# Embedding products ahead of V, sums behind the second V group, the channel matrix and q's scale earlier, in a one-core encoder block

## The chip, the cores and the metric

The kernel runs on one core of one Trainium2 chip. The metric is device time in microseconds: the median of the runs of the whole program. One more run of it was profiled, and all rows shown come from that one. The engines go by the profile's names: PE is TensorE (matrix products; PEld its weight loads), DVE is VectorE, ACT is ScalarE, POOL is GpSimd, SP is the engine whose queue issues most transfers. Every engine works through its own instructions in order, and waits on the others by semaphores.

## The reference

One encoder layer on two sequences of 2048 tokens, 1024 wide, in float32. Attention (8 query heads on 2 key-value heads of width 64) and a Fourier branch run side by side, both are gated, concatenated and projected; then an embedding per token is projected and gated into the stream.

```python
u = _rmsnorm(h, g_norm)
z = u @ w_in                                  # q | k | v | ga | f | gf
...
q = _apply_axial_rope(_rmsnorm(q, g_q), cos, sin)
k = _apply_axial_rope(_rmsnorm(k, g_k), cos, sin)
a = _blocked_gqa(q, k, v) * jax.nn.silu(ga)   # softmax over all 2048 keys
fo = _fourier_branch(f, w_fmix) * jax.nn.silu(gf)
h = h + jnp.concatenate([a, fo], axis=-1) @ w_out
gate = jax.nn.sigmoid(_rmsnorm(h, g_ple) @ w_ple_gate)
return h + (p @ w_ple) * gate
```

A final RMSNorm follows. `_fourier_branch` is the real part of a 2-D DFT over (positions, 64 channels) of each of 8 channel groups, and then a 64 x 64 map per group (`w_fmix`).

## The kernel before, in words

Large products are split into float16 high and low parts, three products for one (`mm`, `SPLIT3`); V, the sums and the DFT are float32. On most engines the order of the instructions is the order in which the program emits them, and a small planner in the program decides that order.

**Projection stage** (`project`). Weights are loaded, their largest value is found (VectorE, then an all-reduce on GpSimd), and they are scaled and split by ScalarE (high half, L334) and VectorE (low half, L335). `weights` is a generator of such steps; `some(wq, 9)` takes nine steps of q's weights. A Newton iteration on VectorE (`newton`, L619 and on) makes the inverse norms of a chunk of rows out of the squares that ScalarE makes (L602). Constants of the Fourier stage are loaded near the end of this stage (`fourier_first`), from a call of `later` in iteration n. The background generator `bg` handles the far weights and, last of all, `channel_map`, which writes the channel matrix `bdd` to DRAM; it comes to its end inside this stage, before iteration n.

**Attention stage** (`attention`, driven by `interleave`). A unit is one tile of 128 queries of one key-value head (4 query heads); there are n = 64 units of 8 steps. In step g = 8u + j TensorE does the scores of a block of 256 keys (L1166, half of the rows at a time, in pairs), and a piece of the maxima for a later unit (L1193, into `ps_m`, which has one buffer; VectorE reduces it, L1201). ScalarE takes exponentials (L1169, two per step), GpSimd adds them up (L1172, L1174). In every fourth step, the heavy one (j = 0 and j = 4), TensorE also multiplies the probabilities of four blocks by V (`pv`, L1229, 32 matmuls, `ps_o`); the group at j = 4 is the first of the unit, the group at j = 0 of the next unit is the second. The sums of exponentials of unit u - 1 (`sums`, L1244) stand ahead of the first group of unit u, in a bank of their own kind (`ps_f`), and `divide` behind them: a reciprocal (L1251) and a product (L1252) on VectorE. One flush later the result is stored (L1255).

**The fill.** In steps that are not heavy, `interleave` lets a second generator add work up to an allowance: FILL = 765 us, shared out over the steps' weights (1, SLOW, RATE, and 0 for a heavy step); what a piece costs, by the program's own estimate, is taken off. The fill is first the second half of the Fourier branch (`fourier2`), then the output projection (`outp`): for each tile t of 128 tokens two slots with `w_out` (out1), two with `w_ple_gate` (out3). A slot has 24 half-row matmuls per half, and the upper half of one slot runs paired with the lower half of the one before (`halves`); pieces end at `STOPS`. Behind an out3 slot ScalarE takes a tanh, and the embedding products are put on a list, `todo`: six full-row matmuls with `w_ple` (`products`, L451, `ps_f`), followed one flush later by two VectorE operations (`last`, L1429 and L1431). `embed` takes them off the list in steps with j = 1, 2 or 7.

**Order by hand.** `defer` puts work on a list that the next step's `flush` emits; `defer_slow` puts long VectorE operations (L1391, L1521, L1535) on another, from which `run_slow` takes two in a heavy step with j = 0 and one at j = 4, ahead of V. `after(ticket)` holds the fill back until something deferred has been emitted. A tile's inputs are loaded (L1368) once both of its units are stored (`ready`). After the last unit the rest of the fill runs alone.

Of the kernel before, what the change touches and what calls it, by code (L numbers as in the profile page):

```python
# [140 lines left out]
class Build:  # L141
    def __init__(self, ctx, tc, a, y):
        self.ctx, self.tc, self.nc = ctx, tc, tc.nc
        self.a, self.y = a, y
        nc = self.nc
        ep = ctx.enter_context
        self.const = ep(tc.tile_pool(name="const", bufs=1))
        self.st = ep(tc.tile_pool(name="st", bufs=2))
        self.psF = ep(tc.tile_pool(name="psF", bufs=1, space=PSUM))
        self.psG = ep(tc.tile_pool(name="psG", bufs=2, space=PSUM))  # L150
        self.grouped, self.last_stores = False, nc.sync
        self.psX, self.nx = None, 0
        self.dq, self.d1, self.nflush, self.bg = None, [], 0, iter(())
        self.slow, self.passed, self.step = [], set(), 0
        self.ahead = iter(())
        self.nw2k = 10
        self.sc = {}
        d = lambda n, s, t: nc.dram_tensor(n, s, t, kind="Internal").ap()
        self.qTd = [d(f"qTd{s}", (NT, 128, 8, 128), F16) for s in range(2)]
        self.kTd = [d(f"kTd{s}", (2, 128, NT // 2, 3, 128), F16) for s in range(2)]  # L160
        self.vd = [d(f"vd{s}", (2, 128, NT, 64), F32) for s in range(2)]
        self.gd = [d(f"gd{s}", (128, NT, 512), F32) for s in range(2)]
        self.gfd = [d(f"gfd{s}", (NT, 128, 512), F32) for s in range(2)]
        self.fod = [d(f"fod{s}", (NT, 128, 512), F32) for s in range(2)]
        self.agd = [d(f"agd{s}", (2, 512, SEQ), F32) for s in range(2)]
        self.bdd = d("bdd", (128, 2, 4, 128), F32)
        self.wd = {}
# [61 lines left out]
    def after(self, ticket, more=0):  # L229
        while self.dq is not None and (ticket[0] is None or self.nflush <= ticket[0] + more):  # L230
            yield None
# [334 lines left out]
    def project(self, P, PU, W, early, later, wkv, wq, wf, wgf, wga, bg, mid):  # L566
# [218 lines left out]
        def iteration(i):  # L785
# [42 lines left out]
            if i == n:  # L828
                later()
# [29 lines left out]
        some(wq, 9)  # L859
# [115 lines left out]
    def fourier_first(self, pool):  # L975

        nc = self.nc
        self.F0 = C, G = {}, {}
        self.cx = pool.tile([128, 128], F32, name="c2x", bufs=1)
        for t in range(FP):  # L980
            C[t] = pool.tile([128, 2, 128], F32, name=f"c2_{t}", bufs=1)
            nc.sync.dma_start(C[t][:].rearrange("p g c -> p (g c)"), self.a["c_dft2"][t])
            for g in range(2):
                G[t, g] = pool.tile([128, 512], F32, name=f"g_in{t}{g}", bufs=1)
                r = 16 * t + 8 * g
                nc.sync.dma_start(G[t, g][:], self.gd[0][r:r + 8].rearrange("r t d -> (r t) d"))
            if t == 0:
                nc.sync.dma_start(self.cx[:], self.a["c_dft2x"])

    def fourier2(self, pool, hook):  # L990
# [42 lines left out]
        def mix(t, fT, fx):  # L1033

            fo = [w2k("fo") for _ in range(2)]
            for y in (1, 0):
# [7 lines left out]
                if y:  # L1044
                    nc.scalar.activation(fo[1][:], ps[:], AF.Copy)
                    step()
                    yield 0.86

            def both():
                for y in range(2):  # L1050
# [16 lines left out]
        nc.sync.dma_start(self.bd[:], self.bdd)  # L1067
# [5 lines left out]
        for t in range(16):  # L1073
# [8 lines left out]
            for i in range(2):  # L1082
                ps = self.bank()
                for r in range(4):
# [3 lines left out]
                                     AF.Copy, scale=self.sc["h_gf"][:])  # L1088
                hook()
# [5 lines left out]
            if t % 8 == 0:  # L1095
# [4 lines left out]
                for r in range(4):  # L1100
# [3 lines left out]
                                     scale=self.sc["h_gf"][:])  # L1104
                yield 0.86
# [18 lines left out]
    def attention(self, kvp):  # L1124
# [94 lines left out]
        def pv(u, j0):  # L1219
# [11 lines left out]
            if j0 + PVG == 8:  # L1231
                if u == last[s, kv]:
                    for b in range(2):
                        del vt[s, kv, b]
                AT[u] = at = pool.tile([128, 2, 128], F32, name="at", bufs=2)
                nc.scalar.activation(at[:].rearrange("p c q -> p (c q)"), o, AF.Copy, scale=self.sc["a_scale"][:])  # L1236
                del O[u]
# [53 lines left out]
        for g in range(8 * n + 7):  # L1291
# [10 lines left out]
            if j == 4:  # L1302
                if u + 1 < n:
                    max_rows(u + 1)
                if u > 0:
                    ps = self.bank()
                    sums(u - 1, ps[:, 0:256])
                    divide(u - 1, ps[:, 0:256])
            heavy = (g - 1) % PVG == PVG - 1 and 0 <= g - 1 < 8 * n
            if heavy:  # L1310
                self.run_slow(1 if j else 2)
                pv((g - 1) // 8, (g - 1) % 8 - PVG + 1)
# [19 lines left out]
    def mix(self, s, out):  # L1332
# [5 lines left out]
        yield from self.after(self.defer(lambda: self.mix_max(s, m)))  # L1338
        ps = self.bank()
# [4 lines left out]
        nc.vector.tensor_scalar(out=m[:], in0=self.ident[:, 0:64], scalar1=r[:, 0:1], scalar2=None, op0=ALU.mult)  # L1344
        yield from self.after([self.nflush])
        ps = self.bank()
        for e in range(2):
            nc.tensor.matmul(ps[64 * e:64 * e + 64, 0:64], self.ones[:], m[:], start=True, stop=True)
        nc.vector.tensor_copy(mm[:, 0:3], ps[:, 0:3])
        yield None  # L1350
        yield from self.after(self.defer(lambda: out.append(self.mix_scale(s, mm))))

    def outp(self, pool0, ow, open_pool):
# [60 lines left out]
        def out3(t, n):  # L1414
            hT = HT[t]

            def fin(ps):
                sl = slice(n * 512, (n + 1) * 512)
                th = pool.tile([128, 512], F32, name="th", bufs=1)
# [3 lines left out]
                def products():  # L1423
# [11 lines left out]
                    ticket = TK[t] = self.defer(last)  # L1435
# [5 lines left out]
        def slot(up, whole):  # L1441
# [14 lines left out]
            if up is not None:  # L1456
                ps = self.group_bank()
                for i, us in enumerate(self.mm(ps[:], up[0], up[1])):
                    yield us
                    yield from embed(i >= 6)  # L1460
# [3 lines left out]
        def embed(now=False):  # L1464

            if todo and (now or self.dq is None or self.step % 8 in (1, 2, 7)):
                todo.pop()()
# [7 lines left out]
        def halves(up, low):  # L1475
            i = n = 0
            for k in range(8):
                for ia, ib in SPLIT3:
# [5 lines left out]
                    if i in STOPS:  # L1484
                        yield 0.216 * (i - n)
                        n = i
                        yield from embed(i >= 18)
# [74 lines left out]
        def along(g, pr):  # L1562

            for us in g:
                for _ in range(round(us / 0.648) if us else 0):
                    next(pr, None)
                poll()
                yield us
# [57 lines left out]
        todo, held, started, due, tm, tk, t4 = [], [], [], [], [], {}, {}  # L1626
# [53 lines left out]
    def run(self):  # L1680
# [92 lines left out]
        def fill():  # L1773
            self.nw2k = NW
            self.small = C0 = fill_stack.enter_context(pool("C0", side="right"))
            with pool("B", side="right") as B:
                self.bd = B.tile([128, 2, 4, 128], F32, name="bd")
# [93 lines left out]
```

## Time and profile before

| what | value |
|---|---|
| median of 3 runs | 2668.47 us (2668.46 to 2668.82) |
| the profiled execution | 2671.73 us |
| its span, first to last instruction | 2670.0 us |
| mean granted TensorE clock | 0.995 of full speed |
| TensorE busy | 2611.3 us, 98% |
| VectorE, ScalarE, GpSimd busy | 1612.9 (60%), 1184.7 (44%), 1630.1 us (61%) |

How to read the rows: in a timeline a row is start, length, engine, line, operation, output <- inputs, shapes and the count of merged instructions; `[1.31 <-DVE a_mx]` means that the engine idled 1.31 us before it, until that. In the list of waits a row is who waited for whom, total us, times, longest. In a window's row the busy time of PE, PEld, DVE, ACT and POOL with instruction counts is followed by the granted clock, the share of DMA time and GB/s. In a group of instructions the two numbers behind the bar are busy us and the mean ns of one. The time of the span can be put against the end, since the engine that is busy nearly throughout, TensorE, also ends last in the chain of work. Matmuls overlap, so the distance from one start to the next, not the length, is what one costs.

### The profile page before, as it was taken

How to read it: one execution, taken by the hardware profiler on the slowest of the kernel's cores; microseconds unless marked ns; L12 is line 12 of the kernel's file. 1: busy time of each engine (PE TensorE's matmuls, PEld its weight loads, DVE VectorE, ACT ScalarE, POOL GpSimd, SP SyncE). 2: the span in 40 equal slices, each digit the busy share in tenths (PEclk: the TensorE clock that was granted, in tenths of full speed). 3: DMA queues.
4: the chain of work that ended last, by engine and by line, in shares of the span. 5: the costliest groups of instructions: out<-in, count | busy, mean ns of one | idle time of the engine just before them, and what ended most of it. 6: DMA issues, size and time to landing. Idle time of an engine off the chain costs nothing.

```text
span 2670.0 us, 49974 instructions
## 1 busy us (share of the span) xinstructions
PE 2611.3 (98%) x20096; PEld 1400.3 (52%) x20096; DVE 1612.9 (60%) x2300; ACT 1184.7 (44%) x1983; POOL 1630.1 (61%) x1376
## 2 busy tenths in 40 slices
PE   6999999999999999999999999999999999999998
PEld 3565655655556654545555544545544544555443
DVE  7756465565555775565675666665665666556634
ACT  4443243433224554544444544445445444544442
POOL 1233342333336885877877877877777877777760
PEclk9999999999999999999999999999999999999999
DMA  8567576676538772222222223322232332232223
GB/s 251 150 163 202 165 217 178 172 185 154 141 74 257 231 219 72 62 77 62 75 67 59 66 69 97 99 64 70 64 90 60 79 77 70 69 79 76 62 76 73
DMA packets 453386, 305.37 MB, mean 114 GB/s; under 512 B 294273, under 2 KB 394817, under 8 KB 453153
## 3 DMA queue, kind: packets, MB, share of 16 engines
q1 hardware_dynamic: 440240, 260.41, 37.9%
q0 software_dynamic: 12912, 41.77, 4.2%
q8 instruction: 157, 2.57, 0.4%
q14 instruction: 77, 0.62, 0.1%
HBM read 149.50 MB, written 86.51 MB: 88 GB/s over the span
## 4 chain that ended last, share of the span: by engine, by line
PE 49%; DVE 2%; ACT 1%; issue 0%; DMA 0%; DVEq 0%; SPq 0%; ACTq 0%
PE ps_g L1481 19%; PE ps_o L1229 12%; PE ps_s L1166 10%; PE ps_m L1193 3%; PE ps_f L451 3%; PE ps_x L451 2%; PE ps_f L1244 1%; DVE h L1521 0%; DVE a_mx L1201 0%; PE ps_g L451 0%; ACT p L1169 0%; DVE h_hl L1535 0%; ACT sq L1502 0%; DVE ps_f L1429 0%; ACT h_hl L1502 0%
## 5 line engine op out<-in xcount | busy, mean ns | idle before, releaser
L1174 POOL TENSOR_TENSOR acc<-acc,p 128x1024 f32<-128x1024 f32 x384 | 919.4, 2394 | 201.0 <-ACT p L1169 161.5
L1201 DVE TENSOR_REDUCE a_mx<-ps_m 128x1 f32<-128x1024 f32 x498 | 609.2, 1223 | 564.5 <-PE ps_m L1193 555.2
L1169 ACT ACTIVATE p<-ps_s,s_scale 128x512 f32<-128x512 f32 x1024 | 647.3, 684 | 652.6 <-PE ps_s L1166 634.9
L1481 PE MATMUL ps_g<-w_pg,hT 64*128 64x512 f16 x2784 | 492.2, 376 | 1.9 <-DVE h L1407 1.1
L1229 PE MATMUL ps_o<-p,v 128*64 128x256 f32 x4096 | 468.2, 381 | 0.0
L451 PEld LDWEIGHTS <-uc 128*128 128x128 f16 x3072 | 301.7, 98 | 310.0 <-issue 20.4
L1166 PE MATMUL ps_s<-q,k 64*128 64x512 f16 x3072 | 433.0, 378 | 6.1 <-ACT p L1169 5.9
L1229 PEld LDWEIGHTS ps_o<-p,v 128*64 128x64 f32 x4096 | 288.8, 137 | 166.7 <-issue 28.5
L1481 PEld LDWEIGHTS <-hT 64*128 64x128 f16 x2784 | 205.0, 94 | 155.4 <-issue 12.4
L1481 PE MATMUL ps_g<-w_wo,mh 64*128 64x512 f16 x1440 | 259.0, 376 | 1.2 <-DVE seen L1447 1.2
L1481 PE MATMUL ps_g<-w_wo,mT 64*128 64x512 f16 x1440 | 256.2, 376 | 0.0
L1166 PEld LDWEIGHTS <-k 64*128 64x128 f16 x3072 | 150.7, 94 | 200.7 <-issue 76.8
L1193 PE MATMUL ps_m<-k,q 64*128 64x512 f16 x996 | 199.9, 377 | 5.1 <-DVE a_mx L1201 4.8
L1172 POOL TENSOR_TENSOR acc<-p,p 128x1024 f32<-128x1024 f32 x64 | 150.7, 2355 | 64.2 <-ACT p L1169 63.6
L451 PEld LDWEIGHTS <-w_ga 128*128 128x128 f16 x1536 | 148.8, 98 | 33.6 <-issue 11.1
L942 POOL DMA_DIRECT2D gfd<-gt x32 | 19.7, 614 | 223.3 <-DVE gt L970 190.1
L1481 PEld LDWEIGHTS <-mh 64*128 64x128 f16 x1440 | 99.8, 94 | 91.2 <-issue 18.4
L1481 PEld LDWEIGHTS <-mT 64*128 64x128 f16 x1440 | 102.7, 94 | 81.3 <-issue 3.8
L1251 DVE RECIPROCAL ps_f<-ps_f 128x256 f32<-128x256 f32 x63 | 110.6, 1756 | 21.2 <-PE ps_f L1244 21.2
L451 PE MATMUL ps_x<-w_f,uc 128*128 128x512 f16 x480 | 105.9, 379 | 0.0
L451 PE MATMUL ps_x<-uc,w_ga 128*128 128x256 f16 x936 | 105.5, 273 | 0.0
L1236 ACT ACTIVATE at<-ps_o,a_scale 128x256 f32<-128x256 f32 x64 | 30.3, 473 | 167.5 <-PE ps_o L1229 167.5
(326 smaller groups left out, 3182.8 us busy)
## 6 DMA issues: line engine op xcount, KB each, us to landing
q<-qTd SPq DMA_DIRECT2D x256, 64.0 KB, 2.3
ag<-agd SPq DMA_DIRECT2D x64, 256.0 KB, 3.3
out<-h POOLq DMA_DIRECT2D x31, 512.0 KB, 3.0
x<-in_x_prompt SPq DMA_DIRECT2D x16, 512.0 KB, 5.2
gfd<-gt POOLq DMA_DIRECT2D x32, 256.0 KB, 2.6
gd<-ge POOLq DMA_DIRECT2D x32, 256.0 KB, 2.8
w_st<-in_w_out SPq DMA_DIRECT2D x32, 256.0 KB, 3.8
agd<-gat POOLq DMA_DIRECT2D x64, 128.0 KB, 2.8
```

The lines of the kernel that those rows point to most:

```text
L451: self.nc.tensor.matmul(ps, lhs(ia, k), rhs(ib, k), start=(i == 0), stop=(i == 3 * ks - 1))
L1166: nc.tensor.matmul(S[u][e][:], w[sl], q[sl].rearrange("p h q -> p (h q)"), start=j == i == 0, stop=i + 1 == len(todo), skip_group_check=True)
L1169: nc.scalar.activation(p[:, e, :], S[u][e][:], AF.Exp, scale=self.sc["s_scale"][:])
L1172: nc.gpsimd.tensor_tensor(out=ACC[u][:], in0=P[u, 0][:], in1=p[:], op=ALU.add)
L1174: nc.gpsimd.tensor_tensor(out=ACC[u][:], in0=ACC[u][:], in1=p[:], op=ALU.add)
L1193: nc.tensor.matmul(ps[c], Q[u][0][sl, h, :], kt[s, kv, half][sl, :, 0, :], start=True, stop=True)
L1201: nc.vector.reduce_max(MX[u][:, h, half, c:c + 1], x, axis=AX.X)
L1229: nc.tensor.matmul(o[64 * f:64 * f + 64], vt[s, kv, c // 8][:, c % 8, :], p[:, e, f], start=(c == 0), stop=(c == 15))
L1236: nc.scalar.activation(at[:].rearrange("p c q -> p (c q)"), o, AF.Copy, scale=self.sc["a_scale"][:])
L1244: nc.tensor.matmul(ps[64 * e:64 * e + 64], self.ones[:], av[:, e], start=True, stop=True)
L1251: nc.vector.reciprocal(r, r)
L1481: nc.tensor.matmul(g[0][:], g[1](ia, k)[sl], g[2](ib, k)[sl], start=a, stop=z, skip_group_check=True)
```

## The change

1. *Products.* In a heavy step, `attention` itself takes one group of embedding products off `todo` (now shared as `self.todo`), right ahead of `pv`, if the one before has been dealt with. Its estimate of 1.48 us is put on `self.owed`, which `along` adds to the next piece of fill. `embed` now takes products only when a second group is waiting, when `middle` asks for them, or after the attention. The tanh gets two buffers (`th`).
2. *Sums.* `pv` runs `sums(u - 1)` behind the second V group of unit u, in the free half of `ps_o`, and defers `divide` by one flush. Only the last unit keeps the old place.
3. *Channel matrix.* `bd` is loaded in `fourier_first`. To make room the constants of tile 1 (`c2`) and one of its inputs (`g_in`) are loaded where `bd` was, at the start of `fourier2`.
4. *q's scale.* `some(wq, 10)` takes one step more: the five VectorE operations of the scale now come ahead of the second `newton`.

The further edits (`del ps`, `box`, `evicted`, the counter of banks) keep track of who holds a PSUM bank.

```diff
             if i == n:
+                self.drain(bg)
                 later()
...
-        some(wq, 9)
+        some(wq, 10)
         newton(None, 1, None)
...
         for t in range(FP):
-            C[t] = pool.tile([128, 2, 128], F32, name=f"c2_{t}", bufs=1)
-            nc.sync.dma_start(C[t][:].rearrange("p g c -> p (g c)"), self.a["c_dft2"][t])
+            if t == 0:
+                C[t] = pool.tile([128, 2, 128], F32, name=f"c2_{t}", bufs=1)
+                nc.sync.dma_start(C[t][:].rearrange("p g c -> p (g c)"), self.a["c_dft2"][t])
             for g in range(2):
+                if t and g:
+                    continue
...
             if t == 0:
                 nc.sync.dma_start(self.cx[:], self.a["c_dft2x"])
+                self.bd = pool.tile([128, 2, 4, 128], F32, name="bd", bufs=1)
+                nc.sync.dma_start(self.bd[:], self.bdd)
...
-        nc.sync.dma_start(self.bd[:], self.bdd)
+        for t in range(1, FP):
+            load_c(t)
+            load_g(t, 1)
...
+                r = O.pop(u)[:, 256:512]
+                if u:
+                    sums(u - 1, r)
                 AT[u] = at = pool.tile([128, 2, 128], F32, name="at", bufs=2)
                 nc.scalar.activation(at[:].rearrange("p c q -> p (c q)"), o, AF.Copy, scale=self.sc["a_scale"][:])
-                del O[u]
+                if u:
+                    self.defer(lambda: divide(u - 1, r))
...
-                if u > 0:
+                if u == n:
                     ps = self.bank()
                     sums(u - 1, ps[:, 0:256])
                     divide(u - 1, ps[:, 0:256])
...
                 self.run_slow(1 if j else 2)
+                if self.todo and self.tk[0] is not None and self.nflush > self.tk[0]:
+                    self.todo.pop(0)()
+                    self.owed += 1.48
                 pv((g - 1) // 8, (g - 1) % 8 - PVG + 1)
...
-                th = pool.tile([128, 512], F32, name="th", bufs=1)
+                th = pool.tile([128, 512], F32, name="th", bufs=2)
...
-            if todo and (now or self.dq is None or self.step % 8 in (1, 2, 7)):
-                todo.pop()()
+            if todo and (now or self.dq is None):
+                yield from self.after(self.tk)
+            if todo and (now or self.dq is None):
+                todo.pop(0)()
                 yield 1.48
...
-                        yield from embed(i >= 18)
+                        yield from embed(len(todo) > 1)
...
+                if us:
+                    us += self.owed
+                    self.owed = 0.0
                 yield us
```

More of the change, by code (lines that the diff above doesn't have):

```diff
@@ L154, in __init__ @@
         self.slow, self.passed, self.step = [], set(), 0
+        self.todo, self.owed, self.tk = [], 0.0, [-1]
         self.ahead = iter(())
@@ L230, in after, with evicted @@
         while self.dq is not None and (ticket[0] is None or self.nflush <= ticket[0] + more):
+            yield None
+    def evicted(self):
+        while self.tk[0] is None:
             yield None
@@ L1045, in mix @@
                     nc.scalar.activation(fo[1][:], ps[:], AF.Copy)
+                    del ps
                     step()
                     yield 0.86
+            box = [ps]
+            del ps
             def both():
+                ps = box.pop()
                 for y in range(2):
@@ L1088, in fourier2 @@
                                      AF.Copy, scale=self.sc["h_gf"][:])
+                del ps
                 hook()
@@ L1104, in fourier2 @@
                                      scale=self.sc["h_gf"][:])
+                del ps
                 yield 0.86
@@ L1308, in attention @@
                     divide(u - 1, ps[:, 0:256])
+                    del ps
+                self.nx += 1
             heavy = (g - 1) % PVG == PVG - 1 and 0 <= g - 1 < 8 * n
@@ L1338, in mix @@
         yield from self.after(self.defer(lambda: self.mix_max(s, m)))
+        yield from self.evicted()
         ps = self.bank()
@@ L1344, in mix @@
         nc.vector.tensor_scalar(out=m[:], in0=self.ident[:, 0:64], scalar1=r[:, 0:1], scalar2=None, op0=ALU.mult)
+        del ps
         yield from self.after([self.nflush])
+        yield from self.evicted()
         ps = self.bank()
@@ L1349, in mix @@
         nc.vector.tensor_copy(mm[:, 0:3], ps[:, 0:3])
+        del ps
         yield None
@@ L1434, in products @@
                     nonlocal ticket
-                    ticket = TK[t] = self.defer(last)
+                    ticket = TK[t] = self.tk = self.defer(last)
                 return products
@@ L1459, in slot @@
                     yield us
-                    yield from embed(i >= 6)
+                    yield from embed(i >= 6 or len(todo) > 1)
                 yield from self.after(ticket)
@@ L1625, in outp @@
         ticket = [-1]
-        todo, held, started, due, tm, tk, t4 = [], [], [], [], [], {}, {}
+        todo, held, started, due, tm, tk, t4 = self.todo, [], [], [], [], {}, {}
         self.grouped = True
@@ L1776, in fill @@
             with pool("B", side="right") as B:
-                self.bd = B.tile([128, 2, 4, 128], F32, name="bd")
                 ow = {}
```

## The prediction

> **What bounds the kernel now.** I read the page's busy times first, then one window over the steady part of the attention stage, then what TensorE waited for, then the timelines of single stretches.
>
> ```profile
> PE 2611.3 (98%) x20096; PEld 1400.3 (52%) x20096; DVE 1612.9 (60%) x2300; ACT 1184.7 (44%) x1983; POOL 1630.1 (61%) x1376
> ...
> 1070.00:2600.00 1530.00, 1523.16 (x13212) 763.37 (x13207) 930.23 (x866) 745.60 (x1226) 1170.60 (x987) 1.00 0.28 73
> ...
> PE ps_x L451 <- ACT wr_q L334: 7.1, 1, 7.1
> ...
> PE ps_g L1041 <- DMA bd<-bdd: 4.8, 1, 4.8
> PE ps_m L1193 <- DVE a_mx L1201: 4.8, 9, 1.3
> ```
>
> TensorE sets the time: 1523.16 of 1530 us busy in the long stage. Its work there is fixed, so a change gains only by dearer-than-needed switches between kinds of matmul or by single waits, and every microsecond in which TensorE is made to wait is added to the end. The two waits that this change names are 7.1 and 4.8 us. The last row matters most below: the maxima (L1193) have one PSUM buffer, so each must wait for VectorE's reduction of the one before (L1201); that costs 4.8 us in all today.
>
> **Embedding products in front of V.** The products are 57 groups of six full matmuls in this form (x342):
>
> ```profile
> L451 PE MATMUL ps_f<-wp,pT 128*128 128x512 f16 x342 | 83.7, 381 | 0.0
> ...
> 1504.43 0.38 PE L1193 MATMUL ps_m<-k,q 64*128 64x512 f16 x2
> 1504.74 1.47 PE L451 MATMUL ps_f<-wp,pT 128*128 128x512 f16 x6
> 1506.14 0.82 PE L1166 MATMUL ps_s<-q,k 64*128 64x512 f16 x6
> 1506.80 0.38 PE L1193 MATMUL ps_m<-k,q 64*128 64x512 f16 x2
> 1507.01 1.46 PE L1481 MATMUL ps_g<-w_wo,mT 64*128 64x512 f16 x12
> ```
>
> Between two kinds that use half rows, a maximum takes 1507.01 - 1506.80 = 0.21 us of TensorE; ahead of a product it takes 1504.74 - 1504.43 = 0.31. The six products take 1506.14 - 1504.74 = 1.40 instead of 6 x 0.216 = 1.30 (twelve half matmuls, six pairs, take the same 1.30). So a group of products pays 0.10 on the way in and 0.10 on the way out. Placed in front of V, the way in remains and one of two ways out is shared: V's own entry. Whether full rows to V's half columns is free the stretch does not show: between 0 and 0.10 saved on top of 0.095, so -5.4 us (57 x 0.095) to -10.8. I take -5.4, because V is again another shape of the array. (The Trainium skill, TensorEngine Tiling (Array Packing), Key Properties, says that changing the tiling mode drains TensorE, while changing the tile does not. Full to half columns is a change of mode, so by that rule the saving is 5.4 and not 10.8; the rows above agree that a change of rows costs about 0.1.)
>
> The price lies in the debt. Before, a product was charged 1.48 to the step in which it ran, where it also gave ScalarE time. Now the charge (owed) falls on the first piece of projection after the V step. A step's allowance is 765 / 420.9 = 1.82 us (the 420.9 is the weighted step count in run), or 2.09 with RATE; the pieces of a slot hold 12, 6, 6, 6, 6, 12 matmuls (STOPS), so in 4 of 6 cases the first piece costs 0.65 + 1.48 = 2.13 and the step ends with six matmuls.
>
> ```profile
> 821.64 0.82 PE L1166 MATMUL ps_s<-q,k 64*128 64x512 f16 x6
> 822.49 1.26 ACT L1169 ACTIVATE p<-ps_s,s_scale 128x512 f32<-128x512 f32 x2
> ```
>
> The exponentials begin 0.85 after the scores and take 1.26: the banks are free 2.11 us after the scores began. Scores 0.65, maximum 0.22 and six matmuls 0.65 fill only 1.51 of that, so TensorE idles 0.60. 57 x 4/6 x 0.60 = **+23 us** (0 if the pieces mostly fall at twelve, 34 if always at six).
>
> **Sums behind the second V group.** Sums and V already stand side by side:
>
> ```profile
> 1523.39 0.65 PE L1244 MATMUL ps_f<-acc,ones 128*64 128x256 f32 x4
> 1523.87 3.62 PE L1229 MATMUL ps_o<-p,v 128*64 128x256 f32 x32
> 1524.63 1.76 DVE L1251 RECIPROCAL ps_f<-ps_f 128x256 f32<-128x256 f32 x1
> 1526.48 0.42 DVE L1252 TENSOR_TENSOR at<-at,ps_f 128x256 f32<-128x256 f32 x1
> ```
>
> so the four matmuls cost the same 0.43 to 0.48 in the new place: 0. What moves is VectorE's work. Today the reciprocal and product (1526.90 - 1524.63 = 2.27 us) run while TensorE does 3.6 us of V. Deferred behind the second group, they come one flush later, in the step after that V, ahead of that step's reduction; nothing long runs on TensorE then. And in that V step run_slow emits two long operations instead of one. This is the place where VectorE is already late:
>
> ```profile
> 1536.65 3.67 PE L1229 MATMUL ps_o<-p,v 128*64 128x256 f32 x32
> 1540.26 0.82 PE L1166 MATMUL ps_s<-q,k 64*128 64x512 f16 x6
> 1540.91 0.38 PE L1193 MATMUL ps_m<-k,q 64*128 64x512 f16 x2
> ...
> 1544.54 0.39 PE L1193 MATMUL ps_m<-k,q 64*128 64x512 f16 x2 [1.31 <-DVE a_mx L1201]
> 1535.63 0.70 DVE L1429 SCALAR_TENSOR_TENSOR ps_f<-th,ps_f 128x512 f32<-128x512 f32 x1 [0.24 <-PE ps_f L451]
> 1536.37 0.75 DVE L1431 SCALAR_TENSOR_TENSOR h<-ps_f,p_wp,h 128x512 f32<-128x512 f32 x1
> ...
> 1538.16 2.98 DVE L1535 SCALAR_TENSOR_TENSOR h_hl<-h,h_r,h_hl 128x1024 f16<-128x1024 f32 x1
> 1541.07 2.29 DVE L1521 SCALAR_TENSOR_TENSOR h<-h,rsh_z,gfin 128x1024 f32<-128x1024 f32 x1
> ```
>
> Here VectorE is busy until 1543.36, 3.1 us past the end of V, and TensorE waits 1.31 us. Put the sums (+0.43 us) and 2.27 us of VectorE's work in this stretch and the reduction starts 2.27 later, the maximum is due 0.43 later: 1.8 us more. Without long operations: the reciprocal starts 0.6 us after V's end, the reduction is done at 0.6 + 2.27 + 1.22 = 4.1 us, and TensorE gets to its second maximum at 0.43 + 0.66 + 0.22 + f + 0.65, with f the projection between: a stall where f is under about 2.1 us. I did this sum for each of the 54 second V groups from here
>
> ```profile
> 1059.60 3.67 PE L1229 MATMUL ps_o<-p,v 128*64 128x256 f32 x32
> ...
> 2502.24 3.67 PE L1229 MATMUL ps_o<-p,v 128*64 128x256 f32 x32
> ```
>
> (the first and the last), with f and VectorE's end as they stand: 24 without a long operation behind V stall 0.22 on average, 16 with one 0.56, 14 with two 1.48: 5.4 + 9.0 + 20.7 = 35, of which about 2.6 are there today: **+32 us**. Where a product ran in front of that V, its two operations (0.70 + 0.75, above) also come ahead of the divide; with them the same sums give 5.4 + 18.7 + 41.0 = 65. About half of the products will fall on a second group: half of the difference, **+15** (0 to 30). No other engine covers any of this: TensorE is in order, and scores and projection stand behind the waiting maximum.
>
> The store of the divided rows also comes 5 steps later; what that may cost is a rival.
>
> **Channel matrix early.** Before, its load stands behind the last k store on SP; two other loads, c2 and g_in of tile 1, now take that place.
>
> ```profile
> 826.69 0.32 SPq L1067 DMA_DIRECT2D bd<-bdd x1
> 823.60 1.06 PE L1085 MATMUL ps_f<-c,g_in 128*128 128x128 f32 x8
> ...
> 830.47 0.79 PE L1041 MATMUL ps_g<-bd,fT 128*128 128x128 f32 x2 [4.85 <-DMA bd<-bdd]
> c<-in_c_dft SPq DMA_DIRECT2D x3, 128.0 KB, 3.4
> 800.00:876.00 76.00, 70.86 (x544) 48.80 (x544) 43.88 (x61) 36.67 (x62) 50.38 (x35) 0.96 0.87 255
> ```
>
> TensorE needs tile 1's c at 823.60, earlier than it needed bd. Issued at 826.69 and 3.4 us on the way, c lands at 830.1: the stall of 4.85 does not go, it moves forward, and the 2.0 us of work between 823.60 and the old stall now comes after it. 830.1 + 2.0 - 830.47 = +1.6; part of that runs at the lowered clock (mean 0.96 in this window), so **+1.8** (0 to +3.6). If c were in time the whole wait and some clock would be saved, -7; that needs an issue 6 us earlier, and SP is not free earlier.
>
> **q's scale sooner.** VectorE leaves the scale chain until behind the second Newton, which waits for ScalarE's squares:
>
> ```profile
> 25.73 0.35 POOL L322 PARTITION_ALL_REDUCE p_mm<-w_m  x1 [9.99 <-DVE n_ms L619]
> 28.45 0.17 DVE L621 TENSOR_SCALAR n_ms<-n_su 128x2 f32<-128x2 f32 x1 [2.79 <-ACT jk L602]
> ...
> 30.91 0.15 DVE L272 TENSOR_SCALAR p_p<-p_mm 128x1 f32<-128x1 f32 x1
> ...
> 32.49 2.74 DVE L335 SCALAR_TENSOR_TENSOR wr_q<-w_z,w_gs,wr_q 128x512 f16<-128x512 f32 x4 [0.79 <-ACT wr_q L334]
> ```
>
> The maximum is ready at 26.1, and the 0.8 us chain fits into VectorE's wait of 2.79. Then ScalarE can split behind its squares, and VectorE's first low half starts when Newton is done, at 31.0 instead of 32.49: **-1.5 us**. The loads behind it on SP move along, so I keep all of it (0 to -2.5).
>
> **Sum**, against the profiled execution of 2671.73 us: -5.4 + 23 + 32 + 15 + 1.8 - 1.5 = +65, so 2737; the median of the runs is 3.3 lower, 2734.
>
> **Rivals.**
> *VectorE has the room* (faster). If f behind the second V group is over 2.1 us nearly everywhere and the debt ends in pieces of twelve, the 70 us are not paid: -5.4 - 1.5 + 1.8 = -5, 2663; with free entry to V and c in time, 2650. For it speaks VectorE's idle share of 40%; against it, the 1.31 us wait above and 30 of 54 groups with long operations. Deciding point: f = 2.1 us. Chance 0.11, and 0.04 that it ends within 0.2% (what a measurement can tell from no change).
> *The debt costs nothing, the divide does* (slower, less): 23 and half of 15 fall away, 2704. For it, ScalarE is idle 51% of the stage. Chance 0.2.
> *The later store starves the projection* (slower, more). Each tile's load stands right behind a store:
>
> ```profile
> 2045.64 0.38 SPq L1255 DMA_DIRECT2D agd<-at  x1
> ...
> 2047.54 0.38 SPq L1368 DMA_DIRECT2D ag<-agd  x1
> 2074.47 1.33 DVE L1391 SCALAR_TENSOR_TENSOR mh<-ag,mix_s,mh 128x1024 f16<-128x1024 f32 x1
> 2075.95 0.38 PE L1481 MATMUL ps_g<-w_wo,mh 64*128 64x512 f16 x1
> ```
>
> This tile is used 1.5 us after its split; five steps of some 3.4 us are 17 us late. In most other tiles I find 14 to 21 us of room. Four bare steps cost about 1.2 us each (2.11 - 0.87); with six such tiles +29, and idle windows that halve the clock for 3.4 us (1.7 us each) may double it: 2763 to 2790. (The Trainium skill, TensorE: Matmul & The Clock Gate, What's actually happening, tells of such a free-running window of 3.4 us; the mean of 0.96 above is of that kind.) Chance 0.15.
> *As forecast:* 0.5, from 2704 to 2765.
>
> The numbers: faster 0.11, same 0.04, slower 0.85. The range leaves out the faster rival and the far end of the worst: 2682 to 2782; the forecast's own is 2704 to 2765.
>
> **What would show it.** Right: TensorE's wait for a_mx (L1201) rises from 4.8 to some 50 us, its wait for p (L1169) to some 25, both right behind a second V group; c instead of bd ahead of L1085 near 823; wr_q's first split at 28.5 on ScalarE. Wrong: those waits under 15 us, or reciprocals that start before V ends.

## The result, and the profile after

The changed kernel takes **2785.93 us** (median of 5 runs, 2779.15 to 2788.06) against 2668.47: a ratio of 1.0429, 95% interval 1.0414 to 1.0443, or +114 us. The forecast was 2734, the end of its range 2782. The direction was right, nearly half of the loss was not in the sum. The profiled execution took 2788.06.

Three views of the changed kernel: the busy times on its page, the waits of TensorE (in all, times, longest), and its busy times in the stretches that the prediction read, with two of the tail (the eighth column is the granted clock).

```profile
PE 2657.8 (95%) x20096; PEld 1430.6 (51%) x20096; DVE 1608.9 (58%) x2300; ACT 1184.4 (43%) x1983; POOL 1630.4 (59%) x1376
```

```profile
PE ps_m L1213 <- DVE a_mx L1221: 39.8, 50, 2.7
PE ps_s L1186 <- ACT p L1189: 34.3, 88, 3.0
...
PE ps_g L1516 <- DVE seen L1480: 6.3, 2, 5.1
PE ps_f L1103 <- DMA c<-in_c_dft: 5.6, 1, 5.6
```

```profile
1070.00:2600.00 1530.00, 1465.39 (x12424) 746.54 (x12420) 881.98 (x828) 705.08 (x1159) 1102.60 (x932) 0.99 0.27 68
...
2600.00:2720.00 120.00, 111.60 (x837) 52.44 (x836) 49.78 (x48) 45.01 (x72) 71.12 (x66) 0.91 0.30 78
2697.10:2717.40 20.30, 17.69 (x41) 5.58 (x41) 7.78 (x10) 3.65 (x5) 1.89 (x2) 0.50 0.55 139
```

In the stretch 1070 to 2600, TensorE's 1523.16 busy us have become 1465.39: 57.8 us lost in the long stage. The wait for the maxima's reduction went from 4.8 to 39.8 us (some 50 were expected), and 39.0 us of it stand behind a second V group, as forecast. The wait for the exponentials went from 8.0 to 34.3 us; its row before the change:

```profile
PE ps_s L1166 <- ACT p L1169: 8.0, 22, 2.3
```

Neither explains TensorE's own 46.5 us of extra "busy" time. Part of that is the clock: the span's mean went from 0.995 to 0.985, which is 28 us over 2786 at most, since TensorE was idle in some of it. What the rest is, the rows do not say. One piece is in the last row: for 20.3 us the tail ran at half the clock, from within a wait for `seen` (VectorE's one-column copy out of a slot's bank), which VectorE reached late:

```profile
2699.71 2.72 PE L1516 MATMUL ps_g<-w_pg,hT 64*128 64x512 f16 x6 [5.14 <-DVE seen L1480]
```

What happens behind a second V group is seen in one stretch of the changed kernel's timeline (start, duration, engine, operation, tiles):

```profile
1141.75 1.47 PE L456 MATMUL ps_f<-wp,pT 128*128 128x512 f16 x6
...
1143.15 3.67 PE L1249 MATMUL ps_o<-p,v 128*64 128x256 f32 x32
...
1147.85 0.38 PE L1213 MATMUL ps_m<-k,q 64*128 64x512 f16 x2
...
1152.88 0.39 PE L1213 MATMUL ps_m<-k,q 64*128 64x512 f16 x2 [2.72 <-DVE a_mx L1221]
```

```profile
1142.99 2.97 DVE L1570 SCALAR_TENSOR_TENSOR h_hl<-h,h_r,h_hl 128x1024 f16<-128x1024 f32 x1
1145.88 2.29 DVE L1556 SCALAR_TENSOR_TENSOR h<-h,rsh_z,gfin 128x1024 f32<-128x1024 f32 x1
1148.10 0.68 DVE L1462 SCALAR_TENSOR_TENSOR ps_f<-th,ps_f 128x512 f32<-128x512 f32 x1
1148.82 0.75 DVE L1464 SCALAR_TENSOR_TENSOR h<-ps_f,p_wp,h 128x512 f32<-128x512 f32 x1
1149.48 1.76 DVE L1275 RECIPROCAL ps_o<-ps_o 128x256 f32<-128x256 f32 x1
1151.27 0.42 DVE L1276 TENSOR_TENSOR at<-at,ps_o 128x256 f32<-128x256 f32 x1
1151.61 1.22 DVE L1221 TENSOR_REDUCE a_mx<-ps_m 128x1 f32<-128x1024 f32 x1
```

This is the queue that the prediction drew: two long operations, the product's two, the divide, and only then the reduction for which the second maximum waits 2.72 us. Product to V takes 1143.15 - 1141.75 = 1.40 us, as product to scores did: the way into V still costs 0.10 (1.40 is also the median of all 56 groups of products in front of V), so one switch is saved and not two. (The Trainium skill, TensorEngine Tiling (Array Packing), Key Properties, says that a change of the tiling mode drains TensorE; by that rule the way from full rows to V's half columns is not free, and this row agrees.)

The stretch that the sum did not contain, in the same timeline:

```profile
1180.94 0.38 SPq L1279 DMA_DIRECT2D agd<-at  x1
1182.84 0.38 SPq L1401 DMA_DIRECT2D ag<-agd  x1
...
1195.69 1.89 PE L1516 MATMUL ps_g<-w_pg,hT 64*128 64x512 f16 x16
1197.42 0.81 PE L1186 MATMUL ps_s<-q,k 64*128 64x512 f16 x6
...
1215.31 2.09 DVE L1424 SCALAR_TENSOR_TENSOR mh<-ag,mix_s,mh 128x1024 f16<-128x1024 f32 x1
...
1217.67 0.39 PE L1516 MATMUL ps_g<-w_wo,mh 64*128 64x512 f16 x1
```

The tile's load again stands 1.9 us behind a store, but it is needed as soon as it is split (1215.31 to 1217.67). From 1197.4 to 1217.6 there is no output projection at all. Stretches of 18 to 22 us like this one begin at 1197, 1507, 1974, 2035, 2094 and 2153 us, with shorter ones between.

### The profile page after: what moved, and what is told of

It reads as the page before. It is cut to its first block, busy times and chain, and to the rows that moved or that the text cites. A ratio compares the mean times of both kernels' runs of the same rounds, so it can differ in the third digit from the quotient of the medians.

```text
span 2785.9 us, 49981 instructions
## 1 busy us (share of the span) xinstructions
PE 2657.8 (95%) x20096; PEld 1430.6 (51%) x20096; DVE 1608.9 (58%) x2300; ACT 1184.4 (43%) x1983; POOL 1630.4 (59%) x1376
## 4 chain that ended last, share of the span: by engine, by line
PE 82%; DVE 10%; ACT 3%; DMA 2%; issue 1%; SPq 1%; POOL 0%; DVEq 0%; ACTq 0%; POOLq 0%
PE ps_g L1516 20%; PE ps_x L456 16%; PE ps_o L1249 15%; PE ps_s L1186 10%; PE ps_g L456 7%; PE ps_f L456 7%; PE ps_m L1213 3%; DVE ps_o L1275 3%; DVE a_mx L1221 2%; ACT p L1189 2%; DVE h L1556 1%; PE ps_o L1268 1%; PE ps_x L931 1%; DVE at L1276 1%; ACT at L1259 1%
## 5 line engine op out<-in xcount | busy, mean ns | idle before, releaser
L1516 PE MATMUL ps_g<-w_pg,hT 64*128 64x512 f16 x2784 | 498.8, 379 | 9.7 <-DVE seen L1480 5.1
L1186 PE MATMUL ps_s<-q,k 64*128 64x512 f16 x3072 | 461.7, 382 | 31.6 <-ACT p L1189 31.4
L1186 PEld LDWEIGHTS <-k 64*128 64x128 f16 x3072 | 164.5, 94 | 239.0 <-issue 120.2
L1213 PE MATMUL ps_m<-k,q 64*128 64x512 f16 x996 | 212.7, 382 | 40.4 <-DVE a_mx L1221 39.8
L1275 DVE RECIPROCAL ps_o<-ps_o 128x256 f32<-128x256 f32 x63 | 111.2, 1765 | 119.9 <-ACT at L1259 119.9
L1516 PEld LDWEIGHTS <-mh 64*128 64x128 f16 x1440 | 105.4, 95 | 86.4 <-issue 22.1
L1516 PEld LDWEIGHTS <-mT 64*128 64x128 f16 x1440 | 111.2, 94 | 65.1 <-issue 0.7
L1213 PEld LDWEIGHTS <-q 64*128 64x128 f16 x1024 | 69.1, 95 | 120.2 <-issue 73.6
```

The costliest lines, as they stand in the source:

```text
L1186: nc.tensor.matmul(S[u][e][:], w[sl], q[sl].rearrange("p h q -> p (h q)"), start=j == i == 0, stop=i + 1 == len(todo), skip_group_check=True)
L1213: nc.tensor.matmul(ps[c], Q[u][0][sl, h, :], kt[s, kv, half][sl, :, 0, :], start=True, stop=True)
L1275: nc.vector.reciprocal(r, r)
L1516: nc.tensor.matmul(g[0][:], g[1](ia, k)[sl], g[2](ib, k)[sl], start=a, stop=z, skip_group_check=True)
```

## The experiments

In what follows a time is the kernel's ratio to the kernel before in the same comparison, times 2668.5 us, with the 95% interval. The theory at the outset: divide, debt and later store each cost by themselves. The rival: one of them makes the loss and the others hide.

**q's scale alone.**

```
-        some(wq, 9)
+        some(wq, 10)
```

> The kernel before with the single change of q's scale (its chain one instruction sooner in the start). The whole change came out 117 us slower; this part is one that I had priced at a gain. Theory A (as forecast): TensorE's first wait for wr_q is over sooner and the rest moves along, -1.5 us (-2.5 to 0) against the kernel before. Theory B (the gain is eaten): in the changed kernel TensorE waits 5.48 us at 30.39 and once more 2.06 us at 33.03 for VectorE's half of wr_q, and half the clock from 27.8 lasted 10.24 us in place of 6.83 us from 29.5; the first scores came 1.2 us sooner in all. Then 0 to -0.8 us here. Both say no slower.

Measured: ratio 1.0000 (0.9991 to 1.0008), 0 us (-2.4 to +2.1). TensorE's waits in that stretch, in this kernel:

```profile
PE ps_x L451 <- ACT wr_q L334: 3.4, 1, 3.4
PE ps_x L451 <- DVE wr_q L335: 2.3, 1, 2.3
```

The first wait is 3.7 us shorter (7.08 before), the second, 0.21 before, is 2.3: VectorE's half is late next. About 1.6 us of gain in the rows, and the times cannot tell that from nothing.

**The channel matrix alone.** The matrix is loaded with tile 0's inputs, two of tile 1's take its old place:

```
+        self.bd = pool.tile([128, 2, 4, 128], F32, name="bd", bufs=1)
+        nc.sync.dma_start(self.bd[:], self.bdd)
...
-        nc.sync.dma_start(self.bd[:], self.bdd)
+        for t in range(1, FP):
+            load_c(t)
+            load_g(t, 1)
```

> The kernel before with the channel matrix loaded early, and nothing else of the change. Theory A (as forecast): the wait of 4.85 us for bd goes and one of about 5.6 us for c of tile 1 comes in its place, 2 us earlier: +1.8 us (0 to +3.6). Rival: the wait is the same length and stands at another place, 0 within 0.5 us, or the clock gets a window less at half, -1.7 us.

Measured: 1.0012 (1.0004 to 1.0021), +3.2 us (1.1 to 5.6). The wait for `bd` is gone, and one for `c` stands in its place, as in the forecast, which had +1.8 (0 to 3.6):

```profile
830.81 1.40 PE L1093 MATMUL ps_f<-c,g_in 128*128 128x128 f32 x5 [5.49 <-DMA c<-in_c_dft]
```

**The sums alone, and the late store alone.** The first is the sums' part of the diff without the products. The second keeps everything of the kernel before and only makes the store wait for five more flushes:

```
-            self.defer(store)
+            def later(k):
+                self.defer(store if k == 0 else lambda: later(k - 1))
+            later(5 if u < n - 1 else 0)
```

> The kernel before with only the sums of exponentials moved behind the second V group, the divide deferred one flush behind it, and so the store of the divided rows five steps later. The products stay where they were and are charged to their own step. Theory A (the divide stands by itself, as the forecast has it): VectorE's reciprocal and product stand ahead of the reduction of the maxima, TensorE's wait for a_mx goes from 4.8 to about 35 us, and the later store adds starved projection of 10 to 25 us: 2705 to 2735. Rival B (debt and divide only cost together): the steps behind V keep all of their projection here, which hides the divide; a_mx stays under 15 us, and the time is within 10 us of the kernel before. Rival C (the store alone): a_mx under 15 us, but projection gaps of some 20 us at several tiles with empty steps, 2690 to 2700.

> The kernel before with only the store of the divided rows made five flushes later (not for the last unit); sums, divide, products and all else as before. Theory A (the later store starves the projection by itself): the room of 14 to 21 us between a tile's split and its first use shrinks to some 0 to 5 us, TensorE has no projection in 15 to 40 steps, each about 1.2 us: +15 to +40, so 2683 to 2708, with more waits for p and more half-clock windows but a_mx as before. Rival B (the room is enough as long as no time is lost elsewhere): within 3 us of the kernel before, the tiles' splits only move closer to their use; the gaps in the changed kernel are then a consequence of its other losses or of where its projection stood.

Measured: the sums alone 1.0310 (1.0294 to 1.0326), **+83 us**, more than theory A's 2735 allows; the late store alone 1.0186 (1.0172 to 1.0200), **+50 us**. Waits and the tail's window of the late store:

```profile
PE ps_s L1166 <- ACT p L1169: 22.1, 59, 2.0
...
PE ps_g L1484 <- DVE mh L1394: 8.5, 8, 1.9
...
PE ps_g L1484 <- DVE seen L1450: 6.3, 2, 5.2
...
PE ps_m L1193 <- DVE a_mx L1201: 3.0, 7, 1.2
```

```profile
2600.00:2721.00 121.00, 106.77 (x574) 46.60 (x570) 42.68 (x96) 28.70 (x44) 27.87 (x34) 0.89 0.30 73
```

The reduction is on time, TensorE even waits for the tile's split itself (`mh`), and the projection has gaps up to 23 us. In 16 of 30 tiles the split's low half begins 3 us or less before the tile's first use; before the change one tile was that tight. The last V matmul starts 38 us later (2624.0 against 2586.0); the other 14 us of this profiled execution (span 2721.7) lie behind it, where the 5.2 us wait for `seen` and a clock of 0.89 stand as in the changed kernel. Rival B is out: this part alone costs as much as the divide and more. The range given for theory A (15 to 40) was still too low.

**A smaller delay.** The same edit with two flushes in place of five.

> The kernel before with only the store of the divided rows later, by two flushes instead of the five of the earlier run (+49 us). Theory A (room: most tiles have 14 to 21 us between split and first use, two steps take about 7 of them): only the few tiles with 1.5 to 7 us of room come late, 0 to +10 us. Rival B (the price grows with each step of delay): 2/5 of 49, +15 to +25.

Measured: 1.0047 (1.0031 to 1.0064), +12.5 us (8 to 17). Two of five steps cost a quarter of the price, between the two expectations. There is room, but it isn't a threshold that the tiles share: p waits are already 16.6 us in place of 8.0, and 9 of 30 tiles have 3 us or less left, where one had before.

**The late divide alone.** The kernel before with the sums in the free half of V's bank, in front of the first V group, and the divide deferred by one flush (the store, which follows the divide, is then one step late, not five):

```
             o = O[u][:, 0:256]
+            if j0 == 0 and u:
+                r = O[u][:, 256:512]
+                sums(u - 1, r)
+                self.defer(lambda: divide(u - 1, r))
```

> The kernel before with only the divide late: the sums stay in front of the first V group, now in the free half of V's bank, and the divide is deferred by one flush, so it follows behind V; the store is one step later, not five. Products as before. Theory A (the divide has a price of its own, 82 us of the sums alone less 49 of the later store): +25 to +35, a_mx about 30 us, no projection gaps over 12 us. Rival B (divide and store cost mostly together): under +15, and then the store's share in the changed kernel is larger than its run alone showed. Rival C: +40 or more, the divide is the larger part.

Measured: 1.0105 (1.0090 to 1.0120), **+28 us** (24 to 32). Without the five steps of the store the divide still costs, and 50 + 28 is nearly the 83 of the sums alone. The 28 contain one step of later store, which no run prices by itself (one gap of 16 us in the projection is there, at 2087 us). But a_mx is only 16.5 us here against 39.9 with the sums alone; the rows of this kernel and of the sums alone:

```profile
PE ps_m L1193 <- DVE a_mx L1201: 16.5, 27, 1.8
```

```profile
PE ps_m L1193 <- DVE a_mx L1201: 39.9, 51, 2.6
```

The timelines show one reason; first this kernel, behind a first V group, then the changed kernel, behind a second one:

```profile
1105.05 0.82 PE L1166 MATMUL ps_s<-q,k 64*128 64x512 f16 x6
1105.16 1.77 DVE L1255 RECIPROCAL ps_o<-ps_o 128x256 f32<-128x256 f32 x1 [2.82 <-PE ps_o L1233]
```

```profile
1202.20 3.67 PE L1249 MATMUL ps_o<-p,v 128*64 128x256 f32 x32
...
1206.24 0.82 PE L1186 MATMUL ps_s<-q,k 64*128 64x512 f16 x6
1206.86 1.77 DVE L1275 RECIPROCAL ps_o<-ps_o 128x256 f32<-128x256 f32 x1 [2.99 <-ACT at L1259]
```

Behind the first group the reciprocal starts 0.11 us after the scores, behind the second 0.62: there it waits for ScalarE to read V's half of the same bank, which in turn waits for the sums.

**The store nearly on time in the changed kernel.** The same edit on the changed kernel, products and debt kept. It brings the store back to one step late, and with it moves the sums and the divide behind the first V group.

> The changed kernel, but the sums of unit u-1 go into the bank of unit u in front of its FIRST V group, where they stood before the change, and the divide is deferred by one flush as in the change. So VectorE's divide still follows behind a V group instead of lying under it, but the store of the divided rows comes one step later than in the kernel before instead of five. Theory A (three separate prices: the later store 49 us, as its run alone showed; the divide about 33, the rest of the run with the sums alone; products and debt about 32): the starved projection and its p waits go, 40 to 50 us come back, and the divide behind a V group with one long operation instead of two gives back some 5 to 10 more of the a_mx wait: 2725 to 2745, a_mx 25 to 35 us. Rival B (the gaps come from the lost time of divide and debt, the store is not needed for them): at most 15 us come back, 2770 or more. Rival C (the store alone makes the loss, divide and debt hide under the room): 2690 or less, a_mx under 15 us.

Measured: 1.0261 (1.0243 to 1.0278), +70 us: **45 us come back**, as theory A has it. a_mx falls by 11.2 us and p by 8.4, so not all of the 45 has to be the store's. The two waits in that kernel:

```profile
PE ps_m L1213 <- DVE a_mx L1221: 28.6, 45, 1.6
PE ps_s L1186 <- ACT p L1189: 25.9, 82, 1.8
```

**The long operations shared out the other way.**

```
-                self.run_slow(1 if j else 2)
+                self.run_slow(2 if j else 1)
```

> The changed kernel with the long operations of VectorE shared out the other way round: one in front of a second V group, where the divide follows, and two in front of a first one, where none does. Theory A (the long operations ahead of the divide make about half of the a_mx wait, 20.7 of 35 us by my sums over the second groups with two): a_mx falls from 39.8 to 20 to 28 us, 10 to 20 us come back, 2766 to 2776. Rival B (the divide with its own 2.3 us is enough for the wait, long operations or not): a_mx stays above 33 us and the time within 5 us. Rival C (an operation now one V group later is late for its tile): slower.

Measured: 1.0412 (1.0396 to 1.0429), 5 us under the changed kernel with overlapping intervals, a_mx 39.6. Rival B: the long operations ahead of the divide do not make half of the wait, although single stretches such as the one at 1152.88 look like it. They make a little: behind the second groups a_mx falls from 39.0 to 34.7 us, behind the first ones, where two long operations stand now, it rises from 0.7 to 4.9.

**The products alone.** The kernel before with only the products' part of the diff.

> The kernel before with only the products moved in front of V, with their debt (any V group); sums, divide and store stay as before. Theory A (my terms: -5.4 for the switches, +23 for the debt, and nothing from the divide, which stays under V): p waits rise from 8 to some 25 us with room in hand, +10 to +25, so 2680 to 2695. Rival B (the debt costs only together with the late divide and the late store): -5 to +3. Rival C: the 32 us between the sums alone and the whole change all lie here, +28 or more.

Measured: 1.0580 (1.0563 to 1.0596), **+155 us**, more than the whole change and far above theory A. Rival C's "+28 or more" holds it in form, but not for its reason. The wait row and one stretch of this kernel:

```profile
PE ps_f L456 <- DVE at L1264: 82.5, 28, 3.8
```

```profile
1096.35 1.76 DVE L1263 RECIPROCAL ps_f<-ps_f 128x256 f32<-128x256 f32 x1
1098.20 0.42 DVE L1264 TENSOR_TENSOR at<-at,ps_f 128x256 f32<-128x256 f32 x1
...
1098.68 2.40 PE L456 MATMUL ps_f<-wp,pT 128*128 128x512 f16 x6 [2.92 <-DVE at L1264]
```

In front of the first V group, beside which the sums take a rotating bank, the product gets that very bank and waits for the divide, 82.5 us in 28 products. The two parts of the change are coupled. The sums' move into V's bank is what lets the products stand in front of the first group without this wait. So the same again with products in front of the other V group only. (`j == 0` is the second group of a unit; where the expectations of this kernel, and of the same one without the debt below, say "a first V group only", the second is meant.)

```
+                if j == 0 and self.todo and self.tk[0] is not None and self.nflush > self.tk[0]:
+                    self.todo.pop(0)()
+                    self.owed += 1.48
```

> The kernel before with the products in front of a first V group only (never in front of the one next to which the sums take a rotating bank), with the debt. Sums, divide and store as before. With products in front of any V group and the sums in their old bank, TensorE had waited 82.5 us in 28 products for VectorE's divide to give the bank back. Theory A (that was the bank alone; what is left is the debt): no waits of products for the divide, p waits of 20 to 27 us, +8 to +25. Rival B: products in front of V cost 100 us or more for another reason, and the time stays above 2780. Rival C (debt for nothing): -5 to +3.

Measured: 1.0111 (1.0096 to 1.0126), **+30 us** (26 to 34), for 43 products, somewhat above theory A. The waits for p have grown as expected; the wait row of this kernel and its busy times:

```profile
PE ps_s L1178 <- ACT p L1181: 21.8, 68, 1.6
```

```profile
PE 2620.8 (97%) x20096; PEld 1418.5 (53%) x20096; DVE 1611.0 (60%) x2300; ACT 1182.8 (44%) x1983; POOL 1627.7 (60%) x1376
```

46 more waits for p list 13.8 us of idle time. The span grew by 27.4 us (2697.4 against 2670.0): TensorE was idle for 17.9 us more, and its busy time as a whole went up by 9.5 us (2620.8 against 2611.3) at the same count of matmuls and a clock of 0.996. Where these 9.5 us come from is not shown.

**Without the debt.** In the changed kernel, in the one with the store nearly on time, and in the one with products in front of a second V group only (there with 43 for 57):

```
-FILL = 765.0
+FILL = 765.0 - 57 * 1.48
...
-                    self.owed += 1.48
```

> The changed kernel without the debt: a product in front of V is charged to no step, and the total to be shared out over the steps is smaller by the same amount (57 x 1.48 us), so the projection is spread evenly. Theory A (the debt makes the steps behind V short, p waits 34 us against 19 with the sums alone): p waits fall to about 20 us and the a_mx wait falls a little as the second maximum is reached later: 15 to 30 us come back, 2756 to 2771. Rival B (the steps are empty because tiles come late, whatever the charge): within 8 us of the changed kernel. Rival C: the projection pulled forward runs into the late store more often, slower than the changed kernel.

> The changed kernel with the sums in front of the first V group in V's bank and the divide deferred (the earlier run of this: 2742, a_mx 28.6, p 25.9 us), now also without the debt, the total smaller by 57 x 1.48 us. Theory A (the debt is a price of its own): p falls to 12 to 18 us and 10 to 20 us come back, 2722 to 2732. Theory B (cover): p falls and a_mx rises by about as much, as in the changed kernel without the debt (p 34.3 to 16.8, a_mx 39.8 to 56.1): within 8 us of 2742.

> The products in front of a first V group only, sums, divide and store as before the change (the earlier run with the debt: +29 us, p waits 21.8 us), now without the debt: a product is charged to no step and the total to be shared out is smaller by 43 x 1.48 us (43 products stood in front of V there). Theory A (the price is the debt, which puts the loss into one step): p waits fall to about 12 us and half or more of the 29 us comes back, 2668 to 2684. Theory B (the price is the cover: 43 products of 1.4 us have gone out of the short steps into a step in which TensorE was busy anyway, and ScalarE's exponentials stay uncovered by as much wherever the charge falls): p and a_mx waits together stay at 22 to 30 us, 2690 to 2705.

Measured: the changed kernel without the debt 1.0390 (1.0372 to 1.0408), 10 us back, between the two theories; with the store nearly on time 1.0134 (1.0119 to 1.0149), **34 us back**, from +70 to +36, more than theory A's 10 to 20. Waits, first of the changed kernel without the debt, then with the store also nearly on time:

```profile
PE ps_m L1213 <- DVE a_mx L1221: 56.1, 61, 2.9
...
PE ps_s L1186 <- ACT p L1189: 16.8, 43, 1.8
```

```profile
PE ps_m L1213 <- DVE a_mx L1221: 30.2, 42, 2.4
...
PE ps_s L1186 <- ACT p L1189: 9.5, 24, 3.0
```

Where tiles arrive in time, the debt is a price of its own: p falls from 25.9 to 9.5 and a_mx stays. Where the store is late, the one wait only turns into the other (74.1 us together with the debt, 72.9 without). The third kernel, 1.0157 (1.0133 to 1.0181), is 12 us *slower* than with the debt, above the ranges of both theories. Its p falls from 21.8 to 9.0 us, but a_mx rises from 7.0 to 12.1, a wait of 10.7 us for `seen` ends at 2626 us, and two waits for `mr` (the transposed maxima) appear, 7.3 us together. It decides nothing: p does what theory A says, a_mx moves as theory B says, and the time follows neither.

**The divide under V again.** The kernel with the store nearly on time, but with the divide called at once instead of deferred.

```
-                self.defer(lambda: divide(u - 1, r))
+                divide(u - 1, r)
```

> The changed kernel with the sums in V's bank in front of the first V group and the divide at once behind them, so that VectorE divides while TensorE does V and the store goes out in the step in which it did before the change. Products in front of V and their debt stay as changed. Theory A (what is left is products and debt, and the coupling of the banks is gone): a_mx under 10 us, p 20 to 30 us, 2680 to 2705. Rival B (VectorE's divide and TensorE's V in one bank wait for each other): V starts 2 us later at each unit, some 63 x 2.2 us: 2800 or more. Rival C: faster than the kernel before, the products' switches are saved and the debt costs nothing.

Measured: 1.1308 (1.1291 to 1.1325), **+349 us**, rival B. The wait row and one stretch:

```profile
PE ps_o L1253 <- DVE at L1276: 213.3, 63, 8.3
```

```profile
1107.17 1.76 DVE L1275 RECIPROCAL ps_o<-ps_o 128x256 f32<-128x256 f32 x1
1108.96 0.42 DVE L1276 TENSOR_TENSOR at<-at,ps_o 128x256 f32<-128x256 f32 x1
...
1109.44 5.36 PE L1253 MATMUL ps_o<-p,v 128*64 128x256 f32 x32 [2.87 <-DVE at L1276]
```

V, in one half of the bank, waits for the divide in the other: 213.3 us over 63 units. The clock falls to 0.957, which is up to 3019.8 x (0.995 - 0.957) = 115 us more. Of the places tried in V's bank, a divide ahead of V costs far more than one behind it, so with the sums there the late divide is the cheaper of the two.

None of these kernels is measurably faster than the kernel before.

## Why the prediction was right and wrong

- **The sum.** Each part alone: late store 50, late divide 28, products with debt 30, channel matrix 3, q 0. Together 111, against +114 for the whole. The theory of separate prices holds to that extent, and part of the closeness is luck: the 30 are for 43 products and not 57, the 28 contain one step of later store, and the debt costs 34 us where tiles come in time but only 10 in the whole change. That the sum without the store (+65) is near the +70 measured with the store nearly on time is luck too: divide and products' operations were put too high (47, the late divide alone measured 28), debt and switches too low (17.6 against 30).
- **The step that failed**: "The store of the divided rows also comes 5 steps later; what that may cost is a rival." It was in the sum with nothing and cost 50 us. The numbers for it were on the page: 17 us late against 14 to 21 us of room. That leaves -3 to +4 us, which is no room, and still I let "most other tiles" count as safe and took six tiles as late. With the late store 16 of 30 had 3 us or less left. Its rival's time (2763 to 2790) holds the result; its chance of 0.15 did not follow from its own arithmetic. What it also lacked is the tail, 14 of the 50 us.
- **Divide, +32**: measured 28. The rival by which VectorE has the room is out. The working inside it was right in part only: the reciprocal does not start 0.6 us after V's end but about 1.0 (1206.86, with V's last matmul done by 1205.87), since it waits for ScalarE's read of the same bank; and the weight given to the long operations (20.7 of 35) fell with their swap, which took 4.3 us of a_mx from behind the second groups.
- **Products' operations ahead of the divide, +15**: not seen where the forecast put them. a_mx is 39.9 us with the sums alone and 39.8 in the whole change. With the divide behind the first group a_mx does grow with the products, from 16.5 us to 28.6, and stays so without the debt (30.2); no run gives this a time of its own.
- **Debt, +23, and switches, -5.4**: 17.6 together, and 30 for 43 products instead of 57. The mechanism was right, and the idle time nearly (13.8 us of p for 43, where 43 x 4/6 x 0.60 is 17.2). Mis-sized was what comes with it: 4.1 us more of other idle time, and TensorE's busy time rose by 9.5 us where the switches alone should have taken 4 off. The switch rows have the size taken, one of two.
- **The rival by which the debt costs nothing** is out where tiles come in time (34 us back without it), and nearly true where they don't (10 us). The kernel with 43 products, slower without the debt, does not fit either.
- **Channel matrix, +1.8; q, -1.5**: 3.2 (1.1 to 5.6) and 0 (-2.4 to 2.1); the waits moved as described.
- **Signs.** a_mx near 50: 39.8, behind second V groups. p near 25: 34.3, of which only 20.6 stand behind a second group. c in place of bd: yes, for 5.6 us. wr_q's first split on ScalarE at 28.5: 28.4 with q's part alone, 29.6 in the whole change.

Open: that the reciprocal's wait for ScalarE's read makes most of the difference between 39.9 and 16.5 us of a_mx was not tried by itself. Between these two kernels VectorE's backlog also differs (it is over 0.6 us late at the end of V behind 15 groups against 5) and the projection behind V is a little shorter. Why two steps of delay cost a quarter of five, and where TensorE's additional busy time comes from, is not settled either.

## What to carry to other kernels

When a step moves, follow the last thing that it issues (here the store, behind sums, divide and one more flush) to its consumer, and put the shortfall into the sum as soon as delay and room are of one size; a rival with its own arithmetic is a term, not a footnote. Work taken out of a step in which TensorE waits for no one and put beside other TensorE work can leave the lighter steps bare, all the more if its charge falls on the next step: here p fell from 25.9 to 9.5 us without the charge. Before moving an operation into a bank that another engine uses, list who reads and writes that bank: order between engines there can cost more than the switch that was saved.

## What the runs showed of the hardware beyond that

- More waits can come with more than their listed idle time: with 46 more waits for p, which list 13.8 us, TensorE's busy time also grew by 9.5 us (2611.3 to 2620.8) at the same count of matmuls. That the waits cause it is not shown.
- A wait can bring more loss than itself: with the 5.14 us of idle time that end at 2699.71 the granted clock was 0.50 for 20.3 us, 17.7 of them busy, some 9 us more. TensorE was busy without a break from 2699.71 on, and the clock still stayed at half until 2717.5. With the sums alone the same wait, 5.17 us long, came with 6.8 us at half the clock.
- As these programs are ordered, two engines on two halves of one PSUM bank wait for each other: V for the divide (213.3 us over 63 units) and the reciprocal for ScalarE's read (0.5 us later). Whether the chip would need that order no run shows.
